# Shared 2 KB places for diagonals and projection weights, and shorter half layer norms, in a conformer convolution stage

## The chip, the cores and the metric

The kernel runs on one core of one Trainium2 chip. The metric is the time of one execution on the device, in microseconds (us); smaller is better. The engines are named as in the profile: PE (TensorE, the matmuls), DVE (VectorE), ACT (ScalarE), POOL (GpSimd) and SP (SyncE, which issues most DMAs).

## The reference

A trunk of two layers over 512 tokens of width 1024, all in float32. Layer 0 has a half-step feed-forward (FFN), a conformer convolution module and a second FFN; layer 1 has an FFN, stick-breaking attention and an FFN. The change lies in the convolution module:

```python
def layer_norm(x, g, b):
    mu = jnp.mean(xf, axis=-1, keepdims=True)
    xc = xf - mu
    var = jnp.mean(xc * xc, axis=-1, keepdims=True)
    y = xc * lax.rsqrt(var + LN_EPS) * g.astype(jnp.float32) + b.astype(jnp.float32)
...
def conformer_conv(x, w_pw1, b_pw1, w_dw, b_dw, ln_g, ln_b, w_pw2, b_pw2):
    h = x @ w_pw1 + b_pw1
    a, gate = jnp.split(h, 2, axis=-1)
    h = a * jax.nn.sigmoid(gate)
    h = lax.conv_general_dilated(
        h, w_dw[:, None, :].astype(h.dtype),
        window_strides=(1,), padding=[(CONV_WIDTH - 1, 0)],
        dimension_numbers=('NWC', 'WIO', 'NWC'),
        feature_group_count=D_MODEL) + b_dw
    h = jax.nn.silu(layer_norm(h, ln_g, ln_b))
    return h @ w_pw2 + b_pw2
```

So: a first projection to twice the width, a gate, a causal depthwise convolution of 31 taps, a layer norm over the 1024 channels of each token, a SiLU, and a second projection (pw2). The convolution's result joins the residual stream, which the next FFN normalises.

## The kernel before

Channels lie on the 128 partitions, in eight chunks (0 to 7); tokens lie along the free dimension. To keep float32 accuracy every operand of a product is split into a high and a low part of the type fp32r, and a product is three matmuls in a row, high by high, high by low and low by high (`mm3`, L325 to L327; the same lines are met in all stages, so tiles tell them apart). Projection weights were split earlier in the run and wait in DRAM as pairs `aparth` and `apartl`; SP brings them back in units `whi` and `wlo` of 512 KB each, three buffers of either kind.

**The convolution stage** (380 to 571 us of the profiled run) is written as a list of steps to a planner, the class `Plan`. Each step names its engine, an estimated duration, what it reads and writes, and a rank; `Plan.issue` walks time forward, always takes the step that can begin first, keeps count of the buffers (`room`), and so fixes the order on PE, DVE, ACT and POOL. The order on SP is left to the scheduler of the whole program.

The steps, by the names that rows show:

- `pa`, the first projection; `gl`, the gated result, and its parts `glh` and `gll`.
- The 31 taps of a chunk are shared out. On PE a tap is three matmuls by a diagonal matrix `d` (its high and low part, two ACT instructions, L625 and L626, into one of 30 buffers of 1 KB), all adding up in the PSUM tile `pc`; `PE_TAPS` counts these taps per chunk. On POOL a tap is a product `pr` by ACT (L681) and an addition to `ws` (L683), nine or ten taps per chunk. The rest are DVE instructions on `pc` (L694). A DVE addition (L698) makes the chunk's result `y`.
- Chunks 5, 6 and 7 (`HALVED`) are worked in two halves of 256 tokens, so that the norm and the second projection of the first half can start while the second half is convolved. In the first half PE has 9 of their taps each, in the second 14 (`PE_TAPS_2`). A diagonal that was made for the first half is used again in the second.
- `layer_norm(h)` for a half: `dsum` and `dsq` are running sums over chunks (POOL; ACT squares). PE makes token sums `ms` and `mq` (L357). The mean row `pb_lm` is made by splitting `ms` on DVE (L722, L723), four ACT diagonals (L729) and two matmuls (L731). DVE works out the inverse root of the variance (L743 to L754, 25 instructions, most on one column each) in PSUM, splits it (`dp_lr`), ACT makes four diagonals `dg_lr`, and two matmuls spread it as the row `pb_lr`. Then for each chunk: subtract the mean (DVE L760, POOL L762), multiply by `pb_lr` (DVE L770), SiLU (ACT L771), and the two parts `shi` (ACT L773) and `slo` (DVE L774).
- `second(h, ...)`: the second projection, `pp`, 24 matmuls for each of eight output chunks and each half. In the first half each output takes a weight unit (`take`); in the second the outputs go in the order `SECOND`, the first three of them with units still held, the other five after the planner's part with units loaded again.

After that the second FFN of layer 0 starts with `pg`. On PE the order in the first half's end is: taps of chunks 5, 6 and 7, token sums, `pb_lm`, `pb_lr`, then `pp`.

## Time and profile before

| | us |
|---|---|
| median of 3 runs (lowest, highest) | 1960.7 (1958.59, 1962.58) |
| profiled execution, its own time | 1960.59 |
| its span | 1958.9 |
| PE busy in the span | 1916.1 (98%) |
| DVE, ACT, POOL busy | 1089.1, 786.5, 278.7 |
| mean granted TensorE clock | 0.99 |

PE is busy almost all the time, so the table says little by itself. What counts is where the other 43 us are. Busy times overlap from engine to engine, and a row of the timeline gives the start, the duration and the line of an instruction (or of a run of like ones, "x4"), and in square brackets how long its engine was idle before it and what ended that.

### The profile page before, as it was taken

The page shows a single profiled execution, that of the slowest core. Times are in us where ns is not written, and L with a number is a line of the kernel's source. Part 1 is how long each engine was busy: PE and PEld are TensorE (multiplying, and loading weights), DVE is VectorE, ACT ScalarE, POOL GpSimd, SP SyncE. Part 2 cuts the span into 40 slices and gives each one's busy share as a digit, 9 for nine tenths or more (in the row PEclk, how much of TensorE's full clock was granted, in tenths as well). Part 3 has the DMA queues.
Part 4 walks back from the last instruction along what each step waited for, and adds up shares of the span by engine and source line. Part 5 has one row for each costly group of instructions (what it writes and reads, how often), then busy time and mean ns, then how long its engine had stood idle before and what let it go on. Part 6 is the DMA issues. An engine that isn't in the chain of part 4 may idle for free.

```text
span 1958.9 us, 23277 instructions
## 1 busy us (share of the span) xinstructions
PE 1916.1 (98%) x8993; PEld 1594.7 (81%) x8993; DVE 1089.1 (56%) x1666; ACT 786.5 (40%) x1222; POOL 278.7 (14%) x261
## 2 busy tenths in 40 slices
PE   9999999999799999999999999999999999999997
PEld 6888888888788888888888888888888688888885
DVE  6444534599865444345744444468999654344344
ACT  6424323677543223224422222346777633222222
POOL 0112202099500000000000000004543100000000
PEclk9999999999899999999999999999999999999998
DMA  5757746543242333323332333242223123332321
GB/s 197 238 182 237 272 148 232 170 167 129 108 160 94 97 97 93 101 94 95 97 97 97 97 98 97 91 152 72 85 77 97 55 96 97 97 97 87 107 84 67
DMA packets 69630, 237.62 MB, mean 121 GB/s; under 512 B 7952, under 2 KB 8080, under 8 KB 69520
## 3 DMA queue, kind: packets, MB, share of 16 engines
q1 hardware_dynamic: 62032, 209.93, 33.6%
q10 hardware_dynamic: 7488, 26.22, 3.6%
q8 instruction: 70, 1.15, 0.2%
q14 instruction: 40, 0.33, 0.0%
HBM read 202.56 MB, written 29.36 MB: 118 GB/s over the span
## 4 chain that ended last, share of the span: by engine, by line
PE 92%; DVE 4%; ACT 2%; DMA 1%; issue 1%; POOL 0%; SPq 0%; DVEq 0%; ACTq 0%
PE pg L325 16%; PE pg L327 16%; PE pg L326 16%; PE pd L325 8%; PE pd L326 8%; PE pd L327 8%; PE z L960 1%; PE pa L325 1%; PE pa L327 1%; PE pa L326 1%; PE po L325 1%; DMA wlo<-apartl 1%; PE po L326 1%; PE po L327 1%; PE pv L325 1%
## 5 line engine op out<-in xcount | busy, mean ns | idle before, releaser
L234 ACT CAST whi<-raw 128x1024 fp32r<-128x1024 f32 (+2 forms) x305 | 313.1, 1028 | 917.0 <-PE pg L326 379.6
L325 PE MATMUL pg<-xhi_f,whi 128*128 128x512 f32 x1408 | 548.1, 390 | 2.8 <-ACT xhi_f L394 1.5
L326 PE MATMUL pg<-xlo_f,whi 128*128 128x512 f32 x1408 | 547.9, 389 | 1.6 <-DVE xlo_f L395 1.6
L327 PE MATMUL pg<-xhi_f,wlo 128*128 128x512 f32 x1408 | 547.8, 389 | 0.1
L235 DVE TENSOR_TENSOR wlo<-raw,whi 128x1024 fp32r<-128x1024 f32 (+2 forms) x305 | 370.3, 1216 | 64.5 <-ACT whi L234 61.9
L325 PEld LDWEIGHTS pg<-xhi_f,whi 128*128 128x128 f32 x1408 | 264.3, 188 | 60.4 <-ACT xhi_f L394 2.7
L326 PEld LDWEIGHTS pg<-xlo_f,whi 128*128 128x128 f32 x1408 | 264.3, 188 | 57.3 <-DVE xlo_f L395 3.0
L327 PEld LDWEIGHTS pg<-xhi_f,wlo 128*128 128x128 f32 x1408 | 264.3, 188 | 55.4 <-DVE wlo L235 0.5
L326 PE MATMUL pd<-hlo,whi 128*128 128x512 f32 x704 | 273.2, 389 | 0.0
L327 PE MATMUL pd<-hhi,wlo 128*128 128x512 f32 x704 | 272.6, 389 | 0.0
L325 PE MATMUL pd<-hhi,whi 128*128 128x512 f32 x704 | 272.6, 389 | 0.0
L452 DVE TENSOR_TENSOR tu<-pg,r_f 128x512 f32<-128x512 f32 x88 | 60.8, 691 | 262.2 <-PE pg L327 262.0
L468 DVE SCALAR_TENSOR_TENSOR xpar<-pd,xpar 128x512 f32<-128x512 f32 x96 | 66.0, 691 | 242.5 <-PE pd L327 242.5
L450 DVE TENSOR_TENSOR tg<-pg,r_f 128x512 f32<-128x512 f32 x88 | 60.8, 691 | 176.4 <-PE pg L327 176.4
L327 PEld LDWEIGHTS pd<-hhi,wlo 128*128 128x128 f32 x704 | 132.1, 188 | 27.6
L325 PEld LDWEIGHTS pd<-hhi,whi 128*128 128x128 f32 x704 | 132.1, 188 | 27.4
L326 PEld LDWEIGHTS pd<-hlo,whi 128*128 128x128 f32 x704 | 132.1, 188 | 27.3
L859 POOL TENSOR_SCALAR_AFFINE_SELECT tri<-ones 128x128 f32<-128x128 f32 x1 | 0.3, 293 | 716.2 <-DVE tu L453 716.2
L235 POOL TENSOR_TENSOR plo<-praw,phi 128x1024 fp32r<-128x1024 f32 x24 | 57.5, 2397 | 280.7 <-ACT phi L234 279.1
L683 POOL TENSOR_TENSOR ws<-ws,pr 128x256 f32<-128x256 f32 (+1 forms) x90 | 90.7, 1018 | 28.4 <-ACT pr L681 24.6
L694 DVE SCALAR_TENSOR_TENSOR pc<-gl,xpar,pc 128x512 f32<-128x512 f32 (+1 forms) x154 | 91.8, 638 | 2.4 <-PE pc L673 0.7
L234 ACT CAST hhi<-tu 128x512 fp32r<-128x512 f32 x88 | 54.9, 624 | 66.9 <-DVE tu L453 66.9
(261 smaller groups left out, 2482.9 us busy)
## 6 DMA issues: line engine op xcount, KB each, us to landing
raw<-in_gu_dram SPq DMA_DIRECT2D x175, 512.0 KB, 3.5
raw<-in_dna_dram SPq DMA_DIRECT2D x64, 512.0 KB, 3.5
whi<-aparth SPq DMA_DIRECT2D x29, 512.0 KB, 3.5
wlo<-apartl SPq DMA_DIRECT2D x29, 512.0 KB, 4.3
praw<-in_pw_dram SPq DMA_DIRECT2D x24, 512.0 KB, 3.9
aparth<-phi ACTq DMA_DIRECT2D x24, 512.0 KB, 2.7
apartl<-plo ACTq DMA_DIRECT2D x24, 512.0 KB, 3.8
raw<-in_dnb_dram SPq DMA_DIRECT2D x32, 384.0 KB, 3.1
```

The source lines that it names most:

```text
L234: ins = A.copy(dst_hi, src)
L235: (G if on_pool else V).tensor_sub(dst_lo, src, dst_hi.bitcast(F32))
L325: PE.matmul(ps, w[0], x[0], start=first, stop=False)
L326: PE.matmul(ps, w[0], x[1], start=False, stop=False)
L327: PE.matmul(ps, w[1], x[0], start=False, stop=last)
L450: V.tensor_mul(tg, pt[0], rb)
L452: V.tensor_mul(tu, pt[1], rb)
L468: V.scalar_tensor_tensor(res[d], pd, 0.5, res[d], op0=ALU.mult, op1=ALU.add)
L683: add("G", 1.28 * f + 0.1 * half, lambda pr=pr: G.tensor_add(accp, accp, pr()[:, at0]), r=[pr], w=[at_], rank=rank)
L694: add("V", 0.66 * f + 0.06 * half, lambda x=x, q=q: V.scalar_tensor_tensor(pc(), x(), q, pc(), op0=ALU.mult, op1=ALU.add), r=[gl], w=[pc], ...
L859: G.affine_select(out=tri, in_=ones, compare_op=ALU.is_ge, fill=0.0, base=0, pattern=[[-1, P]], channel_multiplier=1,)
L960: PE.matmul(dst, st, m[:, a:b], start=False, stop=True, skip_group_check=True)
```

## The change

**More taps on PE early.** `PE_TAPS` of chunks 5 to 7 goes from 9 to 12 in the first half; POOL's taps stay, DVE has three fewer per chunk. The total of diagonals stays, nine of them are made earlier.

**Places.** The 30 diagonal buffers of 1 KB become 14 tiles of 2 KB per partition (`place`), 3 more in a pool whose tiles are free at the time (`placex`), and 6 halves of the three `raw` weight buffers (`placer`). Each holds two diagonals. When the last diagonals in them have been used, 16 DMAs of 256 KB (`hold`) bring quarter parts of the pw2 weights of outputs 3, 4, 5 and 6 (`HELD`) into `place` and `placex`. They stay there for both halves, so that whole units are loaded only for outputs 0, 1, 2 and 7, and once more for 0.

**The half layer norm.** The mean row `lm` is the product of a matrix of ones with `dsum` and with chunk 7's `y`, in plain fp32 straight from the data; the division by 1024 moves into the instructions that read it. The variance takes 15 DVE instructions of two columns each, with one operand in PSUM in each and the other in SBUF.

**Order.** The first half's projection begins with three outputs at once, `SECOND` changes, and the planner models a port that DVE steps marked `port` and POOL steps share.

```diff
-PE_TAPS = [0, 3, 3, 4, 6, 9, 9, 9]
+PE_TAPS = [0, 3, 3, 4, 6, 12, 12, 12]
 POOL_TAPS = [10, 10, 10, 10, 10, 9, 9, 9]
...
-SECOND = (5, 6, 7, 0, 1, 2, 3, 4)
+SECOND = (1, 2, 7, 3, 4, 5, 6, 0)
+HELD = (3, 4, 5, 6)
...
-E_BUFS = 30
+E_BUFS = 14
+X_BUFS = 3
...
-    def add(self, engine, work, do, r=(), w=(), rank=0):
+    def add(self, engine, work, do, r=(), w=(), rank=0, port=False):
...
                 engine = steps[n][0]
                 t = max(t, free.get(engine, 0.0), now)
-                new = [x.kind for x in steps[n][5] if first[x] == n]
-                if any(room[k] < new.count(k) for k in new):
+                if steps[n][6] and port[1] != engine:
+                    t = max(t, port[0])
...
-        for d in (*range(NC), *SECOND[3:]):
+        for d in (0, 1, 2, 7, 0):
...
+        places = {"e": [cv.tile([P, T], F32R, name=f"place{i}") for i in range(E_BUFS)], "raw": []}
+        places["x"] = [x2.tile([P, T], F32R, name=f"placex{i}", tag="xlo", bufs=NC) for i in range(X_BUFS)]
+        for i in range(3):
+            raw = wp.tile([P, UNIT], F32, name=f"placer{i}", tag="raw", bufs=3).bitcast(F32R)
+            places["raw"] += [raw[:, :T], raw[:, T:]]
+        def place(kind="e"):
+            b = Buf(kind, lambda: places[kind][b.slot])
+            return b
...
-            for t in range(n):
-                if (ch, t) in diags:
-                    continue
+            todo = [t for t in range(n) if (ch, t) not in diags]
+            for i, t in enumerate(todo):
                 q = ch * KW + t
-                d = Buf("e", lambda q=q: cv.tile([P, 2, P], F32R, name=f"d{q}", tag="e", bufs=E_BUFS))
-                def do(d=d, q=q):
-                    A.activation(d()[:, 0], ident, AF.Copy, scale=wdh[:, q : q + 1].bitcast(F32))
-                    A.activation(d()[:, 1], ident, AF.Copy, scale=wdl[:, q : q + 1])
-                add("A", 0.6, do, w=[d], rank=rank)
-                diags[ch, t] = d
+                if i % 2 == 0:
+                    d = place(("e", "e", "e", "raw", "e", "x", "e", "raw")[next(turn) % 8])
+                def do(d=d, q=q, i=i):
+                    for j, x in enumerate((wdh[:, q : q + 1].bitcast(F32), wdl[:, q : q + 1])):
+                        o = (2 * (i % 2) + j) * P
+                        A.activation(d()[:, o : o + P], ident, AF.Copy, scale=x)
+                add("A", 0.6, do, r=[d] if i % 2 else [], w=[("diag", ch, t)] + [d] * (i % 2 == 0), rank=rank)
+                diags[ch, t] = d, i % 2
...
+            sm = cv.tile([P, 8], F32, name=f"sm{h}")
+            mean, square, root = sm[:, 0:2], sm[:, 2:4], sm[:, 4:6]
...
-            lm = row("lm", ms, [ms])
+            lm = bank(f"lm{h}", n)
+            for i, (x, t) in enumerate(((dsum[:, sl], f"dsum{h}"), (None, y7))):
+                add("PE", 0.45, lambda i=i, x=x: PE.matmul(
+                    lm(), ones, y[NC - 1]()[:, sl] if x is None else x, start=i == 0, stop=i == 1),
+                    r=[t], w=[lm], rank=rank)
             lms = cv.tile([P, n], F32, name=f"lms{h}", tag="lms", bufs=1)
-            add("A", 0.4, lambda: A.copy(lms, lm()), r=[lm], w=["lms"], rank=rank)
+            add("A", 0.4, lambda: A.activation(lms, lm(), AF.Copy, scale=1.0 / D), r=[lm], w=["lms"], rank=rank)
             def variance():
-                var, root, t = (mq()[:, a : a + 2] for a in (2, 4, 6))
-                one = [slice(j, j + 1) for j in range(2)]
-                for j in one:
-                    V.tensor_scalar_mul(root[:, j], ms()[:, j], ms()[:, j])
-                for j in one:
-                    V.tensor_scalar(var[:, j], root[:, j], -1.0, mq()[:, j], op0=ALU.mult, op1=ALU.add)
+                var, half, last_ = (mq()[:, a : a + 2] for a in (2, 4, 6))
+                V.tensor_copy(mean, ms())
+                V.tensor_mul(square, ms(), mean)
+                V.tensor_sub(var, mq()[:, 0:2], square)
                 V.tensor_scalar(var, var, 0.0, LN_EPS, op0=ALU.max, op1=ALU.add)
-                first_root(root, var)
-                for _ in range(3):
-                    for j in one:
-                        V.tensor_scalar_mul(t[:, j], root[:, j], root[:, j])
-                    for j in one:
-                        V.tensor_scalar(t[:, j], t[:, j], var[:, j], -0.5, op0=ALU.mult, op1=ALU.mult)
-                    for j in one:
-                        V.tensor_scalar(root[:, j], t[:, j], 1.5, root[:, j], op0=ALU.add, op1=ALU.mult)
-            add("V", 3.4, variance, r=[ms], w=[mq], rank=rank)
-            lr = row("lr", Buf("-", lambda: mq()[:, 4:6]), [mq])
+                V.tensor_scalar(half.bitcast(I32), var.bitcast(I32), 1, None, op0=ALU.logical_shift_right)
+                V.tensor_scalar(
+                    root.bitcast(I32), half.bitcast(I32), -1, 0x5F3759DF, op0=ALU.mult, op1=ALU.add
+                )
+                for i in range(3):
+                    V.tensor_mul(half, var, root)
+                    V.scalar_tensor_tensor(half, half, -0.5, root, op0=ALU.mult, op1=ALU.mult)
+                    V.scalar_tensor_tensor(root if i < 2 else last_, half, 1.5, root, op0=ALU.add, op1=ALU.mult)
+            add("V", 3.2, variance, r=[ms], w=[mq], rank=rank)
+            lr = row("lr", Buf("-", lambda: mq()[:, 6:8]), [mq])
...
-                    add("V", 0.36, lambda yc=yc: V.tensor_sub(yc(), yc(), lm()), r=[lm], w=[yt], rank=rank)
+                    add("V", 0.4, lambda yc=yc: V.scalar_tensor_tensor(
+                        yc(), lm(), -1.0 / D, yc(), op0=ALU.mult, op1=ALU.add), r=[lm], w=[yt], rank=rank)
...
+        def hold(d):
+            part = [place("x" if d == HELD[0] and i < X_BUFS else "e") for i in range(4)]
+            for i, x in enumerate(part):
+                src = apart[2 * NC + d][i % 2][:, i // 2 * T : (i // 2 + 1) * T]
+                add("D", 0.8, lambda x=x, src=src: nc.sync.dma_start(x().bitcast(F32), src),
+                    r=[("diag", ch, t) for ch in range(HALVED, NC) for t in range(PE_TAPS_2[ch])], w=[x], rank=49)
+            weights["2", d] = part
+        def kept(d, k):
+            i = k // 4 * 2
+            return at([x() for x in weights["2", d][i : i + 2]], k % 4 * P, P)
...
+            for d in ds:
+                if h == 0 and d == 7:
+                    add("D", 3.0, fetch, r=[("used", 0, 0)], w=["units2", ("unit", d)], rank=48)
...
-        second(0, (0, 1), 50, True)
-        for d in range(2, NC):
-            second(0, (d,), 50 + d, True)
...
-        second(1, SECOND[:2], 90, False)
-        second(1, SECOND[2:3], 91, False)
+        for d in HELD:
+            hold(d)
+        second(0, (0, 1, 2), 50)
+        for d in range(3, NC):
+            second(0, (d,), 50 + d)
+        second(1, SECOND[:3], 90)
+        add("D", 3.0, fetch, r=[("used", 1, 1)], w=["units2"], rank=90)
+        add("-", 0.0, lambda: None, r=[("used", SECOND[2], 1), *(x for d in HELD for x in weights["2", d])], rank=99)
         with tc.manual_schedule(engines={nc.tensor.engine, nc.vector.engine, nc.scalar.engine, nc.gpsimd.engine}):
             plan.issue()
+        fetch()
+        fetch()
         for d in SECOND[:3]:
             n_f2.chunk(d)
         for d in SECOND[3:]:
-            w = unit()
+            w = None if d in HELD else unit()
```

On PE at the end of the first half, ahead of the second projection, these rows stood before (`pc_256` is a chunk's second half):

```order
L327 MATMUL pc_256_4249<-glh_4022,d_4267 128x256
L731 MATMUL pb_lm_4383<-dg_lm_0_4339,onesr 128x256
L673 MATMUL pc_256_4249<-y0h,mshift 128x256
L731 MATMUL pb_lm_4383<-dg_lm_1_4379,onesr 128x256
L731 MATMUL pb_lr_4416<-dg_lr_0_4406,onesr 128x256
L731 MATMUL pb_lr_4416<-dg_lr_1_4409,onesr 128x256
L325 MATMUL pp_0_4446<-shi_4430,whi_3765 128x256
L326 MATMUL pp_0_4446<-slo_4437,whi_3765 128x256
```

and these stand there now, 10 matmuls of `pc_256` ahead of `pp` being left out behind the last row:

```order
L336 MATMUL pc_256_4316<-gll_4049,place_2900 128x256
L337 MATMUL pc_256_4316<-glh_4035,place_2900 128x256
L757 MATMUL pb_lr_4365<-dg_lr_0_4344,onesr 128x256
L335 MATMUL pc_256_4316<-glh_4035,place_2900 128x256
L336 MATMUL pc_256_4316<-gll_4049,place_2900 128x256
L337 MATMUL pc_256_4316<-glh_4035,place_2900 128x256
L757 MATMUL pb_lr_4365<-dg_lr_1_4350,onesr 128x256
L335 MATMUL pc_256_4316<-glh_4035,placex_2903 128x256
L336 MATMUL pc_256_4316<-gll_4049,placex_2903 128x256
L337 MATMUL pc_256_4316<-glh_4035,placex_2903 128x256
```

The mean row's matmuls have left this place, and taps of the second half now stand ahead of, between and behind the two `pb_lr` matmuls.

On SP, the loads for the second projection after its first two outputs were these (the first half's outputs 3 to 7, then the first reload):

```order
L301 DMA whi_4442<-aparth_2347 128x1024
L301 DMA wlo_4444<-apartl_2349 128x1024
L301 DMA whi_4451<-aparth_2429 128x1024
L301 DMA wlo_4453<-apartl_2431 128x1024
L301 DMA whi_4474<-aparth_2511 128x1024
L301 DMA wlo_4476<-apartl_2513 128x1024
L301 DMA whi_4591<-aparth_2593 128x1024
L301 DMA wlo_4593<-apartl_2595 128x1024
L301 DMA whi_4627<-aparth_2700 128x1024
L301 DMA wlo_4629<-apartl_2702 128x1024
L301 DMA whi_4708<-aparth_2029 128x1024
```

and behind the unit of output 2 these follow now:

```order
L310 DMA wlo_3942<-apartl_2267 128x1024
L813 DMA place_2890<-aparth_2429 128x512
L813 DMA placex_2901<-aparth_2347 128x512
L813 DMA place_2891<-apartl_2431 128x512
L321 DMA raw_4871<-in_gu_dram 128x1024
L813 DMA place_2892<-aparth_2429 128x512
L813 DMA place_2893<-apartl_2431 128x512
L813 DMA place_2887<-aparth_2511 128x512
L813 DMA place_2894<-apartl_2513 128x512
L813 DMA place_2895<-aparth_2511 128x512
L813 DMA placex_2902<-apartl_2349 128x512
L813 DMA place_2896<-apartl_2513 128x512
```

Quarter loads wait for a diagonal's last reader, where a whole unit waited for an earlier output's last matmul; the first weights of the next FFN (`raw` from `in_gu_dram`) stand among them.

## Rows read from the trace of the kernel before

**Rows 1.** Windows: stretch; length, PE, PEld, DVE, ACT, POOL busy; clock; DMA.

```profile
500.00:571.00 71.00, 58.00 (x420) 55.33 (x419) 49.72 (x141) 35.90 (x82) 18.56 (x26) 0.88 0.43 156
504.00:514.00 10.00, 4.29 (x16) 3.70 (x17) 9.67 (x33) 6.81 (x19) 5.24 (x8) 0.50 0.00 0
523.00:528.00 5.00, 4.72 (x27) 4.72 (x28) 0.33 (x1) 0.38 (x1) 0.00 (x0) 0.66 0.96 379
537.00:542.00 5.00, 4.29 (x23) 4.29 (x24) 4.47 (x14) 3.41 (x10) 0.00 (x0) 0.66 0.00 0
542.00:571.00 29.00, 27.64 (x223) 26.81 (x223) 17.65 (x32) 14.84 (x28) 0.00 (x0) 1.00 0.57 201
1260.00:1600.00 340.00, 329.10 (x1734) 274.64 (x1733) 265.49 (x458) 206.98 (x374) 96.45 (x98) 0.99 0.30 91
```

**Rows 2.** Timeline of PE: start, duration, instruction, idle before and its releaser.

```profile
414.39 0.50 PE L701 MATMUL pm<-y0h,mshift 128*128 128x512 f32 x1 [0.36 <-ACT y0h L700]
...
476.96 0.28 PE L325 MATMUL pc<-glh,d 128*128 128x256 f32 x1
...
497.70 0.28 PE L327 MATMUL pc<-glh,d 128*128 128x256 f32 x1
497.82 0.50 PE L357 MATMUL ms<-onesD,dsum 128*128 128x1 f32 x4
...
499.70 0.36 PE L325 MATMUL pc<-glh,d 128*128 128x256 f32 x1
...
501.40 0.38 PE L731 MATMUL pb_lm<-dg_lm,onesr 128*128 128x256 f32 x1 [0.39 <-ACT dg_lm L729]
...
502.39 0.38 PE L731 MATMUL pb_lm<-dg_lm,onesr 128*128 128x256 f32 x1 [0.48 <-ACT dg_lm L729]
507.78 0.87 PE L731 MATMUL pb_lr<-dg_lr,onesr 128*128 128x256 f32 x2 [5.01 <-ACT dg_lr L729]
510.58 0.58 PE L325 MATMUL pp<-shi,whi 128*128 128x256 f32 x1 [1.94 <-ACT shi L773]
511.15 0.58 PE L326 MATMUL pp<-slo,whi 128*128 128x256 f32 x1
...
521.71 0.38 PE L325 MATMUL pp<-shi,whi 128*128 128x256 f32 x1 [0.57 <-DMA whi<-aparth]
...
523.28 0.39 PE L327 MATMUL pp<-shi,wlo 128*128 128x256 f32 x1 [1.07 <-DMA wlo<-apartl]
...
537.71 0.48 PE L731 MATMUL pb_lr<-dg_lr,onesr 128*128 128x256 f32 x1 [2.18 <-ACT dg_lr L729]
...
570.70 0.40 PE L325 MATMUL pg<-xhi_f,whi 128*128 128x512 f32 x1
```

**Rows 3.** Timeline of DVE, about the first half's norm.

```profile
499.87 0.50 DVE L743 TENSOR_SCALAR mq<-ms 128x1 f32<-128x1 f32 x2
...
500.94 0.17 DVE L746 TENSOR_SCALAR mq<-mq 128x2 f32<-128x2 f32 x1
501.14 0.17 DVE L362 TENSOR_SCALAR mq<-mq 128x2 int32<-128x2 int32 x1
...
506.55 0.15 DVE L722 CAST dp_lr<-mq 128x2 fp32r<-128x2 f32 x1
...
513.86 0.76 DVE L774 TENSOR_TENSOR slo<-y,shi 128x256 fp32r<-128x256 f32 x2
...
515.36 1.31 DVE L774 TENSOR_TENSOR slo<-y,shi 128x256 fp32r<-128x256 f32 x2
```

**Rows 4.** Timeline of POOL, its additions for taps and sums.

```profile
490.35 14.07 POOL L683 TENSOR_TENSOR ws<-ws,pr 128x256 f32<-128x256 f32 x18
...
515.42 0.96 POOL L650 TENSOR_TENSOR dsum<-dsum,y 128x256 f32<-128x256 f32 x1 [6.10 <-DVE y L698]
```

**Rows 5.** DMA issues by kind: line, queue, count, KB each, median us to landing.

```profile
whi<-aparth SPq DMA_DIRECT2D x29, 512.0 KB, 3.5
```

More of the change, by code (lines that the diff above doesn't have):

```diff
@@ L117, in add @@
         after.discard(n)
-        bufs = {x for x in (*r, *w) if isinstance(x, Buf)}
-        self.steps.append((engine, work, do, after, (rank, n), bufs))
+        bufs = tuple(dict.fromkeys(x for x in (*r, *w) if isinstance(x, Buf)))
+        self.steps.append((engine, work, do, after, (rank, n), bufs, port or engine == "G"))
         return n
@@ L133, in issue @@
                 follow[m].append(n)
-        ends, free, room = [None] * len(steps), {}, dict(self.room)
+        ends, free = [None] * len(steps), {}
+        room = {k: list(range(n)) for k, n in self.room.items()}
         ready = {n: 0.0 for n in range(len(steps)) if not waits[n]}
@@ L139, in issue @@
                 uses[x] = uses.get(x, 0) + 1
-        order, now = [], 0.0
+        order, now, port = [], 0.0, (0.0, None)
         while ready or freeing:
@@ L145, in issue @@
                 t = max(t, free.get(engine, 0.0), now)
-                new = [x.kind for x in steps[n][5] if first[x] == n]
-                if any(room[k] < new.count(k) for k in new):
+                if steps[n][6] and port[1] != engine:
+                    t = max(t, port[0])
+                new = [x for x in steps[n][5] if first[x] == n]
+                if any(len(room[x.kind]) < sum(y.kind == x.kind for y in new) for x in new):
                     continue
@@ L159, in issue @@
             (t, _), n, new = best
-            engine, work, do, _, _, bufs = steps[n]
-            for k in new:
-                room[k] -= 1
+            engine, work, do, _, _, bufs, ported = steps[n]
+            for x in new:
+                x.slot = room[x.kind].pop(0)
             ends[n] = t + work
             free[engine] = t + work
+            if ported:
+                port = (t + work, engine)
             del ready[n]
@@ L169, in issue @@
                 if not uses[x]:
-                    freeing.append((ends[n] + self.LATE, len(order), x.kind))
+                    freeing.append((ends[n] + self.LATE, len(freeing) + len(order), x.kind, x.slot))
             for m in follow[n]:
@@ L316, in fetch, with unit @@
         ready.append((hi, lo))
-    def unit():
+    def unit(ahead=True):
         w = ready.pop(0)
-        fetch()
+        if ahead:
+            fetch()
         return w
@@ L728, in row @@
                         one = parts[:, 2 * i + b : 2 * i + b + 1].bitcast(F32)
-                        do = lambda dd=dd, b=b, one=one: A.activation(dd()[:, b * P : (b + 1) * P], ident, AF.Copy, scale=one)
-                        add("A", 0.28, do, r=[("parts", name, h)], w=[dd], rank=rank)
+                        dst = lambda dd=dd, b=b: dd()[:, b * P : (b + 1) * P]
+                        do = lambda dst=dst, one=one: A.activation(dst(), ident, AF.Copy, scale=one)
+                        add("A", 0.3, do, r=[("parts", name, h)], w=[dd], rank=rank)
                     add("PE", 0.12, lambda i=i, dd=dd: PE.matmul(pb(), onesr, dd(), start=i == 0, stop=i == 1),
@@ L818, in decoder_kernel @@
             for k in range(NC):
-                mm3(pp, at(w, k * P, P), [x()[:, sl] for x in s[k]], k == 0, k == NC - 1)
+                mm3(pp, kept(d, k) if w is None else at(w, k * P, P), [x()[:, sl] for x in s[k]], k == 0, k == NC - 1)
             V.scalar_tensor_tensor(
```

43 lines of the change are left out of this document (25 added, 18 removed).

## The prediction

> **What bounds the kernel now.** I read the busy table first: PE is busy 98% of the span, so the time is that of PE's own stream, and a change pays only where PE waits or runs slowly, or where it changes what PE executes. The windows by stage then show where that is. From 500 to 571 us PE is busy 58.0 of 71.0 us, 13.0 idle, at a mean clock of 0.88 [rows 1]. The attention stage, which the edit does not touch in the source, has another 340 − 329.1 = 10.9 us [rows 1]. So the change has one place to earn anything: the end of the convolution stage.
>
> There the timeline of PE names the waits [rows 2]. The largest is at 507.78: 5.01 us for the four diagonals of the inverse root (`dg_lr`). Its shadow follows: 1.94 us at 510.58 for the first `shi`, then 0.57 us between two matmuls for the first `slo` (510.58 to 511.15). At 501.40 and 502.39 PE waits 0.39 and 0.48 for the mean's diagonals, at 521.71 and 523.28 it waits 0.57 and 1.07 for pw2 weights, and at 537.71 2.18 for the second half's `dg_lr`. After three of these the granted clock falls: the windows 504–514, 523–528 and 537–542 read 0.50, 0.66 and 0.66, hence partly or wholly the lower level, 1.2 GHz [rows 1]. What that costs: 523–528 holds 27 matmuls in 4.72 busy us where 27 × 0.12 = 3.2 would do, 1.5 us.
>
> I size the whole loss by a floor instead of adding waits, since a wait also drains and refills PE's pipeline. From the first tap of chunk 6 (476.96) to the first `pg` (570.70) are 93.74 us. The taps from 476.96 to 497.70 are 174 steps, so 0.119 us each; I use 0.12. PE's order has 577 matmuls of 256 columns there, 69.2 us, and the token sums take 497.82 to 499.70 = 1.88 us in each half, 3.8 together [rows 2]. Floor 73.0, lost 20.7 us.
>
> **The change part by part.** *More taps on PE.* Nine taps are 27 matmuls, 27 × 0.12 = 3.2 us, on the critical engine and paid in full: nine of them ahead of chunk 6's first tap (1.1 us), 18 behind. The diagonals for them are only made earlier; ACT is busy 35.9 of 71 us from 500 to 571 [rows 1], which tells nothing of the time before, so ACT is a rival's subject below.
>
> *The mean row.* Four `pb_lm` matmuls go (4 × 0.12, in the floor), four plain fp32 products with 256 columns come. The trace has none of that form. Nearest below: two records, as a token sum has (four records are two products), each at 0.12, so 0.24 each. Above: the planner's own cost in the diff, 0.45. I take 0.45, 4 × 0.45 = 1.8 us, the end nearer to what the same product costs in split parts, three matmuls or 0.36. In return the two waits at 501.40 and 502.39 go, and DVE's and ACT's share of that row. The Trainium skill, FP8 and Floating Point Precision, TensorE Precision Notes, says that a true FP32 product makes four passes through the array; by that a product would be 4 × 0.12 = 0.48, an estimate, and the sum 0.1 us worse. No row of this trace shows the passes.
>
> *The variance.* From the first instruction at 499.87 to the cast `dp_lr` at 506.55 are 6.7 us [rows 3], with 21 instructions on single columns. A pair of them takes 0.50; a two-column one is followed by the next after 0.20 (500.94 to 501.14) [rows 3]. Now 13 instructions of two columns follow `mq`, 13 × 0.20 = 2.6. That is 4 us less in each half. From cast to the first `pb_lr` stays 507.78 − 506.55 = 1.23 [rows 2, 3].
>
> *What is late next, first half.* PE reaches chunk 6 at 476.96 + 1.1 (taps) + up to 0.7, because the matmul `pm`, which waited 0.36 at 414.39 [rows 2], stands three matmuls earlier in the order (3 × 0.23): 478.7. To the token sums are 144 matmuls and one `lm` product: 478.7 + 17.3 + 0.45 = 496.4. They need chunk 7's `y`, and that needs POOL, whose additions are as many as before: the eight of chunk 7 out of the 18 from 490.35, 14.07/18 = 0.78 each, end at 496.6 [rows 4]; with DVE's final addition 497.0. So PE waits 0.6 here. `mq` is done at 497.0 + 1.9 = 498.9, the cast at 501.5, `pb_lr` may run at 502.8. PE comes to it after 43 more matmuls and the second `lm`, 498.9 + 0.45 + 5.2 = 504.5. The wait of 5.01 is gone, with 1.7 us to spare. The second `pb_lr` ends near 505.3; before, it ended at 507.78 + 0.87 = 508.65 and `pp` started 1.93 later, `slo` 0.57 after that [rows 2]. So `shi` is there at 507.2, `slo` at 507.8, and PE, through 13 taps at 506.6, waits 1.1 us in all. That is a quarter of what stood there, and I take the clock to hold: from 542 to 571 PE idled 29.0 − 27.6 = 1.4 us in pieces and stayed at 1.00 [rows 1].
>
> *Weights.* The last places come free with the second half's last taps, near 505.5. A 512 KB unit lands 3.5 us after its issue [rows 5], and DMA idles from 504 to 514 (share 0.00, rows 1), so even at a whole unit's latency the quarters are there at 509. Output 3 starts 72 matmuls after 507.8, at 516.4. The waits at 521.71 and 523.28 go, cover 7 us; those of the second half go too, as outputs 1, 2 and 7 keep their units.
>
> *Second half.* PE comes to the token sums at 507.8 + 117 × 0.12 + 0.45 = 522.3 or so; `mq` 524.2, `pb_lr` possible at 524.2 + 2.6 + 1.23 = 528.0, PE there after 42 matmuls and an `lm` product at 529.7. The wait of 2.18 is gone, and the slow clock after it.
>
> *A rule against it.* Two `slo` subtractions take 0.76 together at 513.86, but 1.31 at 515.36, when a POOL addition runs, itself 0.96 instead of 0.78 [rows 3, 4]. Before, POOL stood idle for 6.10 us up to 515.42, just when `slo` was made [rows 4]; now it may be at its additions. At worst DVE needs 1.31/2 + 0.33 = 0.99 a chunk, and PE, with three outputs at once, uses a chunk in 9 × 0.12 = 1.08, so only the first `slo` can cost, up to 0.8; I take nothing and keep that for the range. The Trainium skill, SBUF — State Buffer, SBUF: two separate sides, says why: a DVE instruction with two SBUF inputs and a POOL instruction exclude each other for the whole instruction; the rows agree, and by the rule at its worst the sum is 0.8 us less.
>
> *Sum.* After: 591 matmuls × 0.12 = 70.9, token sums 3.8, `lm` 1.8, waits 0.6 + 1.1, and 0.4 for refills: 78.6 against 93.74, 15.1 gained; the start is 1.1 + 0.7 late. Net 13.3. Profiled execution 1960.59 (the median differs by 0.1) − 13.3: **1947 us**. Ends: `lm` at 0.24, no `pm` delay, no waits, −3.0 (1944); `slo` blocked 0.8 and one slow stretch 1.5, +2.3 (1949.5). Attention's order is dealt anew by the scheduler, sign unknown; I allow a quarter of its 10.9 idle us, ±2.5.
>
> **The rivals.** *POOL or ACT becomes the bound.* ACT now makes all diagonals ahead of the norm, between the products that feed POOL. For it: POOL adds without a pause, 18 in 14.07, so it has no reserve. Against: ACT's products are buffered three deep. If POOL slips over the 1.7 us of spare, each further us returns at `pb_lr`, in both halves. A slip of 4 gives 2 × 2.3 + 1.5 of slow clock back: 1953; with both `dg_lr` waits back in full (5.01 + 2.18 + 2 × 1.5), 1957.
>
> *Held weights come late.* A place waits for the last reader of its diagonals, and SP takes its loads in order. With 7 us of cover; 3 us beyond it are 1947 + 3 + 1.5 = 1951.5.
>
> *Slower.* One quarter load (`place2`) stands in SP's queue ahead of the units of outputs 0, 1, 2. If its place were freed only by late taps, SP would hold the first projection's weights. Decides from 507, when PE wants them; 13.5 + 3.9 us later, about 525, the kernel is slower by 0.2%: 1965. Against it: the place's last reader in PE's order is a tap of chunk 4, far earlier.
>
> *Nothing.* The waits move elsewhere one for one: 1957 to 1964; the floor rises by only 3.3 us, so this needs 10 us of new waits.
>
> *More.* y of chunk 7 earlier and attention in luck: 1938 to 1942.
>
> **How the numbers follow.** Forecast (1942.5–1951) 0.62; POOL or ACT 0.17, of which 0.04 ends at 1957 or above; late weights 0.06, of which 0.02 there; attention costing more than 4 us, 0.04; more 0.07; slower 0.04. Runs can tell about 0.2%, 3.9 us. Faster by more than that 0.90, within it 0.06, slower 0.04. The range 1942 to 1955 leaves out most of "more", the tails of POOL and weights, and slower: about 0.17.
>
> **What would show it.** Right: no wait above 1 us at `pb_lr` in either half, `pg` starting near 557, clock 1.00 between 504 and 542, no DMA wait at `pp` from output 3. An `lm` product between 0.24 and 0.48. Wrong: PE waiting for `y` of chunk 7 or `dsum` by over 2 us; POOL idle between 400 and 497; a `pp` that waits for a place; idle time in attention moved by over 3 us.

## The result and the profile after

The changed kernel takes 1942.8 us (median of 4 runs, 1941.9 to 1944.0) against 1960.2 (4 runs, 1958.6 to 1962.6); the ratio is 0.9911, 95% interval 0.9893 to 0.9928. That is 17.4 us less, where 13.3 were forecast: inside the stated range, near its lower end. The profiled execution of after took 1943.27 us, its span is 1941.6.

The windows of after, in the stretches of [rows 1] (length; busy time of PE, PEld, DVE, ACT, POOL; granted clock; DMA share; GB/s):

```profile
500.00:571.00 71.00, 69.82 (x529) 66.95 (x528) 53.04 (x152) 38.09 (x79) 19.89 (x28) 1.00 0.29 98
504.00:514.00 10.00, 8.90 (x72) 8.49 (x71) 9.28 (x25) 8.88 (x24) 5.37 (x8) 1.00 0.58 196
523.00:528.00 5.00, 5.00 (x44) 4.95 (x43) 2.78 (x17) 0.80 (x2) 1.66 (x3) 1.00 0.00 0
537.00:542.00 5.00, 5.00 (x44) 5.00 (x44) 1.09 (x4) 1.45 (x4) 0.00 (x0) 1.00 0.00 0
```

PE idles 1.2 us of the 71 instead of 13.0, and the granted clock, 0.50 to 0.66 in three of these stretches before, reads 1.00 in all four. PE's timeline of after, at the places of [rows 2]:

```profile
415.62 0.50 PE L724 MATMUL pm<-y0h,mshift 128*128 128x512 f32 x1 [1.10 <-ACT y0h L723]
...
479.95 0.28 PE L335 MATMUL pc<-glh,place 128*128 128x256 f32 x1
...
491.96 0.60 PE L764 MATMUL lm<-dsum,ones 128*128 128x256 f32 x2
...
492.51 0.28 PE L336 MATMUL pc<-gll,place 128*128 128x256 f32 x1
...
497.52 0.50 PE L367 MATMUL ms<-onesD,dsum 128*128 128x1 f32 x4
...
499.22 0.68 PE L764 MATMUL lm<-y,ones 128*128 128x256 f32 x2
...
499.85 0.28 PE L336 MATMUL pc<-gll,place 128*128 128x256 f32 x1
...
504.86 0.28 PE L757 MATMUL pb_lr<-dg_lr,onesr 128*128 128x256 f32 x1
505.34 0.28 PE L757 MATMUL pb_lr<-dg_lr,onesr 128*128 128x256 f32 x1
507.76 0.39 PE L335 MATMUL pp<-shi,whi 128*128 128x256 f32 x1 [0.57 <-ACT shi L803]
508.67 0.39 PE L336 MATMUL pp<-slo,whi 128*128 128x256 f32 x1 [0.52 <-DVE slo L804]
...
530.71 0.28 PE L757 MATMUL pb_lr<-dg_lr,onesr 128*128 128x256 f32 x1
...
557.93 0.40 PE L335 MATMUL pg<-xhi_f,whi 128*128 128x512 f32 x1
```

Neither half waits for the inverse root any more, none of the `pp` waits for a DMA, and what is left between the norm and the projection is 0.57 + 0.52. To see where the whole 17 us lie I cut the execution at the same instructions in each kernel: the first `pa` of the convolution stage, the first `pg` after it, the first `pv` of attention, the first `pg` of the last FFN, and the final `ss_out`. These stage lengths, read from the starts of those rows, carry the rest of the document.

| kernel (profiled execution) | first `pa` at | convolution | two FFNs | attention | last FFN |
|---|---|---|---|---|---|
| before | 372.20 | 198.50 | 720.98 | 289.37 | 360.57 |
| after | 373.36 | 184.57 | 721.04 | 284.80 | 360.60 |
| difference | +1.2 | −13.9 | +0.1 | −4.6 | 0.0 |

The convolution stage gave 13.9 us, attention, of which no source line changed, 4.6; the first 372 us took 1.2 more. Over the kernels below whose activations lie where before has them, the first `pa` stands anywhere from 371.7 to 373.5, so that last figure is scatter. Every length is that of one execution. After, `a_tp256` and `a_tp448` have the same order of instructions and differ in a memory place alone; their convolution stages are 184.6, 183.9 and 184.3, so I draw nothing from a difference under about 1 us there.

### The profile page after: what moved, and what is told of

It reads as the page before. It is cut to its first block, busy times and chain, and to the rows that moved or that the text cites. A ratio compares the mean times of both kernels' runs of the same rounds, so it can differ in the third digit from the quotient of the medians.

```text
span 1941.6 us, 23310 instructions
## 1 busy us (share of the span) xinstructions
PE 1911.4 (98%) x9022; PEld 1596.2 (82%) x9024; DVE 1079.6 (56%) x1633; ACT 784.4 (40%) x1214; POOL 276.1 (14%) x261
## 4 chain that ended last, share of the span: by engine, by line
PE 95%; DVE 2%; ACT 1%; POOL 1%; issue 0%; DMA 0%; SPq 0%; DVEq 0%; ACTq 0%; POOLq 0%
PE pg L337 16%; PE pg L336 16%; PE pg L335 16%; PE pd L337 8%; PE pd L336 8%; PE pd L335 8%; PE z L1016 2%; PE pa L335 1%; PE pa L337 1%; PE pa L336 1%; PE po L335 1%; PE pv L335 1%; PE pq L335 1%; PE pv L337 1%; PE pq L336 1%; PE pv L336 1%
## 5 line engine op out<-in xcount | busy, mean ns | idle before, releaser
L335 PEld LDWEIGHTS pg<-xhi_f,whi 128*128 128x128 f32 x1408 | 265.0, 188 | 59.4 <-ACT xhi_f L400 2.7
L706 POOL TENSOR_TENSOR ws<-ws,pr 128x256 f32<-128x256 f32 (+1 forms) x90 | 91.0, 1024 | 58.2 <-ACT pr L704 54.6
```

The costliest lines, as they stand in the source:

```text
L335: PE.matmul(ps, w[0], x[0], start=first, stop=False)
L706: add("G", 1.28 * f + 0.1 * half, lambda pr=pr: G.tensor_add(accp, accp, pr()[:, at0]), r=[pr], w=[at_], rank=rank)
```

## The experiments

The theory to be tested: the gain of the stage comes from the inverse root that ends sooner, with taps that fill PE's wait for it and held weights behind it, and attention's part from the order in which its matmuls are dealt. The rivals: one part alone (the taps, say) carries it, and attention follows from the state that the stage leaves.

| label | what it is | convolution | two FFNs | attention | ratio to before, interval |
|---|---|---|---|---|---|
| `b_var` | before + new variance | 194.62 | 720.97 | 290.60 | 0.9981 (0.9971 to 0.9990) |
| `b_varlm` | before + new variance and mean row | 193.46 | 735.03 | 287.67 | 1.0055 (1.0040 to 1.0070) |
| `b_varlm_align` | the same, `LEAN_TP` 320 | 192.87 | 721.04 | 283.39 | 0.9948 (0.9932 to 0.9965) |
| `a_oldnorm` | after with the old variance and mean row | 191.06 | 725.94 | 284.51 | 0.9973 (0.9962 to 0.9983) |
| `a_oldvar` | after with the old variance | 190.59 | 721.04 | 288.79 | 0.9942 (0.9927 to 0.9957) |
| `a_oldlm` | after with the old mean row | 183.69 | 721.01 | 284.55 | 0.9909 (0.9892 to 0.9926) |
| `a_taps9` | after with 9 taps | 187.64 | 721.04 | 288.44 | 0.9936 (0.9921 to 0.9950) |
| `a_taps11` | after with 11 taps | 185.88 | 721.04 | 285.16 | 0.9909 (0.9893 to 0.9925) |
| `a_reload` | after, all weights reloaded | 201.15 | 721.11 | 286.44 | 0.9995 (0.9985 to 1.0005) |
| `a_tp256` | after, `LEAN_TP` 256 | 183.89 | 735.02 | 285.59 | 1.0005 (0.9995 to 1.0014) |
| `a_tp448` | after, `LEAN_TP` 448 | 184.27 | 734.89 | 285.87 | 1.0011 (1.0002 to 1.0020) |
| `a_pm16` | after, `pm` later on PE | 184.84 | 721.04 | 286.38 | 0.9906 (0.9891 to 0.9922) |

**The new variance alone.** The edit replaces the body of `variance` in the kernel before, as in the diff:

```diff
-                for j in one:
-                    V.tensor_scalar_mul(root[:, j], ms()[:, j], ms()[:, j])
...
+                V.tensor_copy(mean, ms())
+                V.tensor_mul(square, ms(), mean)
...
```

> The kernel before with the new variance alone (15 two-column DVE instructions). Theory A, the variance is the larger part: the inverse root's row can run 3.8 us sooner, so the first half's wait of 5.01 falls to about 1.2, the second's of 2.18 goes with 1.5 us of slow clock: convolution stage (first pa to first pg of the second FFN) 198.5 - 7.5 = 191 (189.5 to 192.5). Rival, the extra taps are the larger part: what the variance gives is taken back by the waits for shi and slo behind it, stage above 195. Attention (first pv to the last FFN's first pg): PE's order there is that of the kernel before, so 289.4 as before if the order sets it. Time about 1953.

The stage came to 194.6, 3.9 less and not 7.5. DVE's timeline of `b_var` says why, in part:

```profile
502.55 0.17 DVE L754 SCALAR_TENSOR_TENSOR mq<-mq,sm 128x2 f32<-128x2 f32 x1
503.76 0.42 DVE L760 TENSOR_TENSOR y<-y,pb_lm 128x256 f32<-128x256 f32 x1 [1.04 <-ACT lms L739]
504.10 0.15 DVE L724 CAST dp_lr<-mq 128x2 fp32r<-128x2 f32 x1
```

ACT's and PE's rows of the same run go on from there:

```profile
504.98 1.26 ACT L731 ACTIVATE dg_lr<-ident,dp_lr 128x128 fp32r<-128x128 f32 x4
...
506.00 0.88 PE L733 MATMUL pb_lr<-dg_lr,onesr 128*128 128x256 f32 x2 [3.15 <-ACT dg_lr L731]
```

The variance is done at 502.7, but in DVE's order the first subtraction of the mean stands ahead of the split of the root, and waits 1.04 us for the mean row. From the cast at 504.10 to `pb_lr` at 506.00 are 1.90 where before has 1.23, because ACT ends a `pr` product first and begins the diagonals at 504.98. So PE still waited 3.15 for `dg_lr`, where 1.2 was expected, and the 1.93 and 0.40 behind it stayed. The shorter variance uncovered the mean row and ACT.

**Variance and mean row together.** The second edit is that of the diff on `lm`; then the same with the padding constant changed:

```diff
-            lm = row("lm", ms, [ms])
+            lm = bank(f"lm{h}", n)
...
-LEAN_TP, LEAN_DG = 256, 64
+LEAN_TP, LEAN_DG = 320, 64
```

> The kernel before with the new variance and the new mean row. The mean row: waits of 0.39 and 0.48 gone, four plain fp32 products of 0.43 for four matmuls of 0.12, +1.2: stage 0.3 us from that of the variance alone, 191.3 (189.5 to 192.5). PE's order in attention is now that of the changed kernel, though taps, places and held weights are as before. If that order sets attention's length: 284.8, time about 1948.5. Rival, that attention gains from the state it starts in (places, weights, memory): 289.4, time about 1953.

> The kernel before with the new variance, the new mean row and LEAN_TP 320, which brings the activation tiles to the place they have in the kernel before (64 bytes past a multiple of 256). Theory A: FFNs 721.0, convolution stage 191.5 (190 to 193), attention 284.8 as in the changed kernel, whose order on PE it shares there; time about 1949. Rival for the attention, that its length follows the stage before it: 289 to 291. Rival for the FFNs: 735 again.

`b_varlm` was slower than before, by 11 us, and not in the stage (193.5, a little over the 189.5 to 192.5 expected): the two FFNs took 735.0 instead of 721.0. The windows of the same 60 us in an FFN, for before, `b_varlm` and `b_varlm_align` in turn, show PE busy all the time in each, and fewer matmuls in `b_varlm`:

```profile
700.00:760.00 60.00, 60.00 (x266) 49.70 (x265) 26.56 (x32) 17.37 (x21) 0.00 (x0) 1.00 0.32 97
...
700.00:760.00 60.00, 60.00 (x259) 48.35 (x258) 25.51 (x30) 16.13 (x20) 0.00 (x0) 1.00 0.31 93
...
700.00:760.00 60.00, 60.00 (x266) 49.68 (x265) 27.23 (x33) 17.90 (x22) 0.00 (x0) 1.00 0.32 97
```

266 against 259 in the same time at the same clock. A window also counts a matmul that overlaps its edge; from start to start, the step of matmuls of 512 columns is 0.2267 us there in before and 0.2333 in `b_varlm`. It is not so all through the program: the step rises in `pd`, the second product of all four FFNs, and in `pg` of the one FFN right behind the convolution, while `pg` of the other three keeps 0.2267. For the two FFNs behind the convolution that is twice 528 `pd` and 1056 `pg` at 6.7 ns more, the 14.0 us. The new mean row does without some small tiles, and activation tiles behind them moved down by 64 bytes. As I read the compiled programs, which no trace holds, the `xhi_f` and `xlo_f` tiles of this FFN lie 64 bytes past a multiple of 256 in before, on a multiple of 256 in `b_varlm`, and 64 past again in `b_varlm_align`, where `LEAN_TP`, a tile that nobody reads, is 64 bytes larger. With it the FFNs take 721.0 again. The same line stands in the change; see `a_tp256`.

The stage of `b_varlm_align` is 192.9, 5.6 less than before: within what was expected for it (190 to 193).

**The norm as before in the changed kernel.**

> The changed kernel with the old variance and the old mean row. Theory A: the inverse root comes 3.8 us later and the split of the means 0.4 more in each half; PE gets there 0.5 us sooner; spare was 0.9 and 1.4. Waits of 3.8 and 3.2 and twice 1.5 of slow clock, less 1.2 for the cheap mean matmuls: stage 184.6 + 8.8 = 193.4 (190.5 to 195). Rival, taps and held weights carry the gain: under 188. Attention has the changed kernel's order: 284.8. Time about 1952.

> The changed kernel with the old variance alone (25 instructions, most on one column). It ends 3.8 us later in each half, of which 0.9 and 1.4 were spare: waits of 2.9 and 2.4 for the inverse root's row, and 1.5 of slow clock after one or both. Theory A: stage 184.6 + 5.3 + 1.5 = 191.4 (189 to 193.5). Rival, other waits were as late and cover it: under 187. Attention has an order of its own.

> The changed kernel with the old mean row alone (split on DVE, four diagonals by ACT, two matmuls in each half), and LEAN_TP 256, which with the tiles that come back keeps the activations 64 bytes past a multiple of 256. Theory A: the row comes later, and on DVE the first subtraction of it stands ahead of the split of the inverse root, as in the kernel before with the new variance, where it waited 1.04; of that 0.9 and 1.4 are spare, while PE saves 1.2. Stage 184.6 - 1.2 + 0.5 to 2 = 184 to 185.5. Rival, the mean row holds the norm as much as the variance: over 187. FFNs 721, attention 284.8 (same order as the changed kernel).

Edits: the bodies of `variance` and of the mean row exchanged for those of before; in `a_oldlm` also

```diff
-LEAN_TP, LEAN_DG = 320, 64
+LEAN_TP, LEAN_DG = 256, 64
```

`a_oldnorm` was run without that line, and its tiles lie 128 past a multiple of 256: 725.9 for the FFNs, so its ratio mixes two things. Its stage, 191.1, lies in the range that was expected (190.5 to 195). `a_oldvar` is clean, and lands at 190.6, 6.0 us above after and near the middle of what was expected; PE's timeline shows the two waits that came back, 2.10 and 2.08 where 2.9 and 2.4 were expected (the clock fell behind the second alone, to 0.83 from 530 to 540):

```profile
505.78 0.68 PE L762 MATMUL pb_lr<-dg_lr,onesr 128*128 128x256 f32 x2 [2.10 <-ACT dg_lr L760]
...
534.03 0.68 PE L762 MATMUL pb_lr<-dg_lr,onesr 128*128 128x256 f32 x2 [2.08 <-ACT dg_lr L760]
```

`a_oldlm` took 183.7, 0.9 less than after and a little under the 184 to 185.5 expected: with the other parts in place the new mean row gains nothing in the stage. On the kernel before it was worth 194.6 − 192.9 = 1.8. What a part is worth depends on which of the others is there.

**The taps.**

```diff
-PE_TAPS = [0, 3, 3, 4, 6, 12, 12, 12]
+PE_TAPS = [0, 3, 3, 4, 6, 9, 9, 9]
```

> The changed kernel with 9 instead of 12 taps of chunks 5 to 7 on PE in the first half. PE has 3.2 us less to do and comes to the inverse root's row 2.2 sooner, where it had 0.9 to spare; DVE has nine taps of 0.40 more. Theory A, the taps about pay for themselves: waits of 1.3 to 2.5 come back, stage between 183 and 187. Rival, the taps are what hides the norm: over 188. Attention has an order of its own: not told by either.

> The changed kernel with 11 instead of 12 taps of chunks 5 to 7 on PE in the first half: PE has 1.1 us less, DVE three taps of 0.40 more. With 9 taps the stage was 3.1 longer. Theory A, the wait appears only when the spare 0.9 us are used up: stage 183.5 to 184.8. Rival, a loss in proportion: 185.6. Attention 284.8, the changed kernel's order.

With nine the stage fell between the two theories (187.6, against 183 to 187 and over 188), with eleven on the rival's side (185.9, against 185.6 in proportion). So the 3.2 us of matmuls that the change adds here are more than paid: without them the stage is 3.1 longer. PE's timeline of `a_taps9`, and of `a_taps11` behind the line of dots:

```profile
505.64 0.88 PE L757 MATMUL pb_lr<-dg_lr,onesr 128*128 128x256 f32 x2 [3.26 <-ACT dg_lr L755]
508.81 0.58 PE L335 MATMUL pp<-shi,whi 128*128 128x256 f32 x1 [2.29 <-ACT shi L803]
...
506.49 0.38 PE L335 MATMUL pp<-shi,whi 128*128 128x256 f32 x1 [1.73 <-ACT shi L803]
507.37 0.58 PE L336 MATMUL pp<-slo,whi 128*128 128x256 f32 x1 [0.50 <-DVE slo L804]
```

DVE makes chunk 7's `y` and begins the variance in these rows, of after, `a_taps9` and `a_taps11`:

```profile
496.75 0.42 DVE L721 TENSOR_TENSOR y<-pc,ws 128x256 f32<-128x256 f32 x1
499.57 0.15 DVE L772 COPY sm<-ms 128x2 f32<-128x2 f32 x1
...
497.81 0.42 DVE L721 TENSOR_TENSOR y<-pc,ws 128x256 f32<-128x256 f32 x1
501.16 0.15 DVE L772 COPY sm<-ms 128x2 f32<-128x2 f32 x1
...
497.92 0.15 DVE L772 COPY sm<-ms 128x2 f32<-128x2 f32 x1
```

With nine, PE waits 3.26 for the root's row and not 1.3 to 2.5, because DVE, with three more taps a chunk, is late too: counted from the first `pa` it begins this `y` at 125.7 where after has 123.4, and the variance at 129.1 where after has 126.2. With eleven it begins the variance as early as after does (126.1). There is no wait at `pb_lr`; the 1.1 us that PE saves comes back as a wait of 1.73 for `shi` where after has 0.57, and from that `pp` to the first `pg` the stage is 1.1 us longer, at clocks of 0.87 and 0.96 in 500 to 510 and 510 to 520. So, by these rows, the twelfth tap of a chunk fills a wait of PE, and the two before it also take work off DVE ahead of the norm. I had counted only the spare time at `pb_lr`.

**The held weights.** The edit makes `HELD` empty, restores the old `SECOND` and its order of loads, and lets each further output load its unit when an earlier one has been used:

```diff
-HELD = (3, 4, 5, 6)
+HELD = ()
...
-                if h == 0 and d == 7:
-                    add("D", 3.0, fetch, r=[("used", 0, 0)], w=["units2", ("unit", d)], rank=48)
+                if h == 0 and d >= 3:
+                    add("D", 3.0, fetch, r=[("used", d - 3, 0)], w=["units2", ("unit", d)], rank=48)
```

> The changed kernel with no held weights: every output of the second projection loads whole units as before, five of them twice, diagonals still in places. Theory A: the waits for whi and wlo come back, 1.6 in the first half, 1.4 in the second and 1.5 of slow clock: stage 184.6 + 4.5 = 189 (187 to 190.5). Rival, the earlier norm leaves loads enough time by itself: under 186. Attention has an order of its own, neither that of before nor of after: any length between 284 and 292 fits theory A, 284.8 the rival that attention follows the convolution stage.

The stage took 201.2: 16.6 above after, longer than before, where 4.5 were expected. PE's timeline has the waits for weights, the largest in the second half, and one window shows the price of the clock:

```profile
518.25 0.38 PE L335 MATMUL pp<-shi,whi 128*128 128x256 f32 x1 [0.45 <-DMA whi<-aparth]
519.49 0.54 PE L337 MATMUL pp<-shi,wlo 128*128 128x256 f32 x1 [0.74 <-DMA wlo<-apartl]
...
553.37 0.38 PE L335 MATMUL pp<-shi,whi 128*128 128x256 f32 x1 [2.88 <-DMA whi<-aparth]
```

```profile
520.00:530.00 10.00, 10.00 (x48) 9.82 (x47) 4.84 (x23) 2.08 (x6) 3.56 (x6) 0.51 0.47 179
```

From 520 to 530 PE never idles and still runs 48 matmuls, where 10/0.12 = 83 fit: 4.2 us lost at a granted clock of 0.51, the lower level of 1.2 GHz, after waits that sum to 2.7 between 517 and 520 (one of them, 1.53, for POOL's `dsum`). The experiment is harsher than before was, because three outputs begin at once and take all three buffers, so that nothing is loaded ahead. It shows that this order of outputs needs held weights, not what holding them is worth by itself. By difference, before to after is 13.9, variance and mean row give 5.6 on before and the taps 3.1 in after: some 5 are left for places, held weights and order, if the parts add up, and `a_oldlm` shows that they do not quite. No run has held weights alone.

**The place in memory.** One line of the change that the cut of the diff above leaves out:

```diff
-LEAN_TP, LEAN_DG = 256, 64
+LEAN_TP, LEAN_DG = 320, 64
```

> The changed kernel with its padding constant LEAN_TP put back from 320 to 256: the same instructions in the same order on every engine, but the activation tiles that PE streams lie 64 bytes lower per partition. The kernel with the old placing and the new norm had its FFN matmuls of 512 columns at 0.232 us instead of 0.226 and the two FFNs after the convolution at 735.0 instead of 721.0. Theory A, the place in memory does that: the same here, 735, the first and the last FFN 3.6 longer each, attention about 3, so 24 us more, time about 1967. Rival, it came from that kernel's own instructions or state: FFNs 721, time 1943.

> The changed kernel with the activations 128 bytes higher, 192 past a multiple of 256. Seen so far for the two FFNs after the convolution: 0 past 735.0, 64 past 721.0, 128 past 725.9. Theory A, the place in memory alone decides and 64 is the best of those seen: between 721 and 735, stage and attention a little longer if the FFNs are. Rival, a better place is left: under 720, and the whole time below 1940.

`a_tp256` and `a_tp448` have the same instructions in the same order as after on PE, DVE, ACT and POOL. They take 1963.1 and 1963.9, 20 us more than after and no better than before. PE's window in an FFN, for after, `a_tp256`, `a_oldnorm` and `a_tp448`, that is for activations 64, 0, 128 and 192 bytes past a multiple of 256:

```profile
700.00:760.00 60.00, 60.00 (x266) 49.72 (x265) 28.31 (x34) 17.99 (x22) 0.00 (x0) 1.00 0.30 94
...
700.00:760.00 60.00, 60.00 (x259) 48.44 (x258) 27.12 (x32) 17.90 (x22) 0.00 (x0) 1.00 0.29 94
...
700.00:760.00 60.00, 60.00 (x264) 49.23 (x263) 26.65 (x33) 17.87 (x22) 0.00 (x0) 1.00 0.31 97
...
700.00:760.00 60.00, 60.00 (x259) 48.25 (x258) 27.11 (x32) 17.85 (x22) 0.00 (x0) 1.00 0.28 92
```

Full clock, PE busy all the time, and 259 to 266 matmuls. Fifty steps from start to start, in after and in `a_tp256`, give 0.2266 and 0.2332 us each:

```profile
699.73 0.39 PE L336 MATMUL pg<-xlo_f,whi 128*128 128x512 f32 x1
...
711.06 0.39 PE L335 MATMUL pg<-xhi_f,whi 128*128 128x512 f32 x1
...
699.73 0.39 PE L335 MATMUL pg<-xhi_f,whi 128*128 128x512 f32 x1
...
711.39 0.39 PE L337 MATMUL pg<-xhi_f,wlo 128*128 128x512 f32 x1
```

The place that before has, and after keeps by that line, is the best of the four; the better one of the rival is not among them. That the place makes the difference is shown by these edits; by how many bytes it lies past a multiple of 256 is my reading of the compiled programs. The weight units lie at the same place in all of them, so it is the activations' place, alone or against the weights'; which of the two, and why, no run here tells.

**The wait that is left on PE's way.**

```diff
-                add("PE", 0.23, lambda: PE.matmul(pm(), mshift, y0h, start=True, stop=True), r=["y0h"], w=[pm], rank=-1)
+                add("-", 1.6, lambda: None, r=["y0h"], w=["y0h_late"])
+                add("PE", 0.23, lambda: PE.matmul(pm(), mshift, y0h, start=True, stop=True), r=["y0h_late"], w=[pm], rank=-1)
```

> The changed kernel with the matmul pm (chunk 0's carry for the convolution) placed nine matmuls of 512 columns later on PE, where the copy it needs is there: its wait of 1.10 us goes, nothing else is touched. Stage 183.5 (183.2 to 184.2) by both theories, unless DVE's addition that needs pm now comes late and POOL behind it: then 184.6 or more. Attention 284.8, time 1941.5 to 1943.

The wait of 1.10 at `pm` went, and the stage did not shorten (184.8 against 184.6). PE's timeline of `a_pm16` has a new one instead, 70 us further on:

```profile
485.79 0.39 PE L336 MATMUL pc<-gll,place 128*128 128x256 f32 x1 [1.22 <-POOL gll L632]
```

Chunk 7's low part `gll` comes from POOL, which adds without a pause up to there. PE, sooner by 1.1, waits for POOL by 1.2. Neither theory named this place: the second one expected POOL's delay, not its plain lack of reserve. So between `pm` and chunk 7's taps PE has no reserve over POOL: take one wait away and POOL's stands in its place. In the change itself PE never waits for POOL there, so the forecast's rival "POOL becomes the bound" has not come true; it is what bounds the next step.

**Attention.** PE's order there, compared row by row, is one and the same in before and `b_var`; another one and the same in after, `b_varlm`, `b_varlm_align`, `a_oldnorm`, `a_oldlm`, `a_taps11`, `a_tp256`, `a_tp448` and `a_pm16`; and of its own in each of `a_oldvar`, `a_taps9` and `a_reload`. The lengths go by it: 289.4 and 290.6 for the first; 283.4, 284.5, 284.6, 284.8, 285.2 and 286.4 for the second, leaving out the three with the slowest place (285.6 to 287.7); 288.8, 288.4 and 286.4 for the others. In the traces ACT's and POOL's order changes in the same kernels, so "the order" is that of the whole stage. `b_varlm_align` has taps, reloaded weights and a convolution stage as before, 8 us longer than after's, and its attention is 283.4. So neither taps nor held weights are needed for the gain; all six kernels with the new order lie at least 3.0 under both with the old one. Its size is less sure: with one order and one place the lengths spread over 3.0 us, and `b_varlm`, with the order and instructions of `b_varlm_align` at another place, lies 4.3 above it.

PE's waits in the stage sum to 10.9 before and 10.0 after; the rest is busy time (278.5 against 274.8). The window of the stage for `pv` alone (length; busy time of PE, PEld, DVE, ACT; granted clock, DMA share, GB/s), in before, `b_var`, after and `b_varlm_align`, shows where much of it lies:

```profile
1291.68:1581.05 289.37, 59.37 (x384) 53.75 (x383) 9.03 (x32) 8.36 (x32) 0.99 0.28 83
...
1287.49:1578.09 290.60, 59.36 (x384) 53.73 (x383) 9.03 (x32) 8.36 (x32) 0.99 0.28 83
...
1278.97:1563.77 284.80, 54.09 (x384) 50.52 (x383) 9.02 (x32) 8.45 (x32) 0.99 0.29 84
...
1287.43:1570.81 283.38, 54.06 (x384) 50.48 (x383) 9.06 (x32) 8.44 (x32) 0.99 0.29 85
```

The same 384 matmuls are busy 59.4 us in the old order and 54.1 in the new one, to within 0.1 in each. Where one `pv` follows another the step is 0.12 in both; but in before 80 of them are followed by a matmul of another tile, in after 49. That each such change of tile costs PE time is suggested by this and not tested.

## Why the prediction was right, point by point

**The bound.** That the loss lay from 500 to 571 held, and the floor was the right measure: 20.7 us over the floor were forecast to fall to 2.1, and `pg` to start near 557; it started at 557.93. Taken apart, the sum holds: from chunk 6's first tap (479.95) to `pg` are 78.0 where 78.6 were forecast, and that tap is 3.0 late, of which 1.2 is the scatter of the first `pa` and 1.8 was forecast. The 0.6 between them is the wait at the token sums, which did not come. (The new floor is 3.5 over the old one, not 3.3, and the old variance has 22 single-column instructions, not 21; nothing rests on either.) Of the signs named, all came but one: three `lm` products cost more than 0.48.

**More taps.** The cost of 3.2 us of PE was right, the worth was not worked out. By the prediction's own figures, nine taps fewer would save 3.2 and bring back a wait of 3.2 − 1.7 = 1.5 at `pb_lr`, a stage 1.7 shorter; `a_taps9` is 3.1 longer. What that reckoning leaves out is DVE, which with those taps comes 2.9 later to the variance, and the clock, 0.78 and 0.88 in 500 to 510 and 510 to 520 of that run.

**The mean row.** An `lm` product was taken at 0.45. In PE's timeline the next matmul but one starts 0.55 after the product at 491.96 and 0.63 after the one at 499.22; less 0.12 for the matmul between, that is 0.43 and 0.51, and the two of the second half come to 0.53 and 0.51 in the same way. So the four cost 2.0 against 1.8, a little over the upper end. The Trainium skill's four passes (FP8 and Floating Point Precision, TensorE Precision Notes) give an estimate of 4 × 0.12 = 0.48, nearer to the mean of the four, 0.50, than the 0.45 taken; no run shows the passes themselves.

**The variance.** 13 instructions of 0.20 were forecast behind `mq`; DVE's timeline of after has them from 500.02 to 502.59, 2.6. The 4 us in each half is what DVE saved, not what PE did: by `a_oldvar` the new variance is worth 6.0 in the stage for both halves.

**What is late next.** Token sums at 497.0 after a wait of 0.6, measured 497.52 without one, in an execution whose first `pa` is 1.2 late. `pb_lr` at 504.5 without a wait, measured 504.86 without one. The waits for `shi` and `slo` 1.1 together, measured 0.57 + 0.52. Second half: token sums 522.3 (523.46), `pb_lr` 529.7 (530.71), no wait. `pm` was allowed 0.7 more (0.74). The clock held, as taken.

**Weights.** No wait.

**The rule against it.** DVE's and POOL's rows of after:

```profile
507.98 0.97 DVE L804 TENSOR_TENSOR slo<-y,shi 128x256 fp32r<-128x256 f32 x2
...
509.60 0.75 DVE L804 TENSOR_TENSOR slo<-y,shi 128x256 fp32r<-128x256 f32 x2
...
512.54 1.31 DVE L804 TENSOR_TENSOR slo<-y,shi 128x256 fp32r<-128x256 f32 x2
...
512.61 0.96 POOL L673 TENSOR_TENSOR dsum<-dsum,y 128x256 f32<-128x256 f32 x1 [4.27 <-DVE y L721]
```

The first two `slo` took 0.97 against 0.75 for the next pair, in a stretch in which POOL adds: 0.2 us and not 0.8, within the wait of 0.52. The fourth pair took 1.31 beside an addition of 0.96, as before, and PE did not wait for it. The Trainium skill's lock (SBUF — State Buffer, SBUF: two separate sides) agrees with these rows, and the price to PE was small here.

**Where the size was off.** The sum was short by 4.1 us (17.4 against 13.3). The convolution stage gave 13.9 of it, near enough; the term that was off is attention: ±2.5 around nothing, measured −4.6. I had taken a quarter of PE's idle time there as the measure, but the order moved PE's busy time (3.7 of the 4.6) more than its idle time. That attention gained was luck: the prediction had no sign for it.

**What the sum lacked.** `LEAN_TP` had no term at all. It is worth 20 us, more than the whole gain. The forecast came out because that line does what it must: with the old value, `a_tp256`, the change shows no gain at all (ratio 1.0005), for a reason that none of the rivals named. On this point too the forecast was lucky.

## What to carry to other kernels

A wait behind a chain over several engines goes only when each link is shortened to the next engine's own bound: the variance alone gave 3.9 us, with the mean row 5.6, with the taps, places, held weights and order of the whole change 13.9. Read what each engine executes just ahead of the link (DVE's taps, ACT's products, a subtraction that waits for another row) before pricing the link by its own length. And when tiles are added or taken away, compare the pitch of matmuls in a stage that should not have changed: it tells at once whether the memory place of their operands has moved.

## What the runs showed of the hardware that was not expected

Matmuls of 512 columns in the FFN behind the convolution, in a stream without waits and at full clock, started every 0.2267 us with activations 64 bytes past a multiple of 256, every 0.2289 at 128 and every 0.2333 at 0 and at 192 (mean steps from 700 to 760 us in after, `a_oldnorm`, `a_tp256` and `a_tp448`): 2.9% more for the place of a tile. And a short row of waits, 2.7 us in all from 517 to 520 in `a_reload`, was followed by ten microseconds at a granted clock of 0.51, which cost 4.2 us, more than the waits did.
